# Hybrid decoder layer: sparse pairs begun among the u tiles, K=64 spreads of h2, gate rows on GpSimd, 56 dense columns

## The chip, the cores and the metric

One NeuronCore of a Trainium2 chip runs the whole layer in one launch. The metric is the device time of one execution in microseconds (us); the median of the runs is given.

## The reference, cut to what matters

The layer has a mixer (sparse attention and a short convolution) and then a retrieval FFN, called PEER. The change lies in the second half and in the load of one modulation vector, `gate2`.

```python
mod = silu(c) @ w_ada + b_ada          # shift1, scale1, gate1, shift2, scale2, gate2
...
h2 = rms_norm(x, norm2_w) * (1.0 + scale2) + shift2
x  = x + gate2 * peer_ffn(h2, ...)

# peer_ffn, for each of 256 tokens and 8 heads (16384 experts = 128 x 128):
q = h2 @ peer_wq                        # two halves of 128 a head
s = q . peer_subkeys                    # 128 scores for each half
vals, idx = top_k(s, 16)                # of each half
combo = vals0[:, None] + vals1[None, :] ; ids = idx0 * 128 + idx1
top_s, pos = top_k(combo, 16)           # 16 experts of the head
g = softmax(top_s)
a = gelu(peer_u[expert] . h2)           # rows of 1024
out = sum over heads and experts of g * a * peer_v[expert]
```

Each token so uses 8 x 16 = 128 experts, each with a row of `peer_u` and a row of `peer_v`, in float32.

## The kernel before

Expert e = 128 i + j has a column number j. The experts are split by j in two parts.

**Dense part, j < J0 = 64.** For each j, all 128 experts with that j are computed for all 256 tokens. `u_tile(j)` loads 512 KB of `peer_u` and multiplies it with `h2f` (h2 transposed, float32) on TensorE, 8 products of 128x128 by 128x256; ACT takes the GELU of it into `B0[:, j]` (`evict`, lines 1039 and 1042). `g_step` spreads the softmax weights of four tokens at a time (`GT = 4`, so 64 groups) over i and j: ACT and DVE make one-hot tiles `oi` and `oj` (lines 1074 to 1077), TensorE multiplies them (line 1065), DVE multiplies the result into `B0` (line 1055). One `g_step` follows each u tile; the groups left over are done in a loop behind the u tiles (lines 1194 to 1196). Then `v_tile(j)` loads 512 KB of `peer_v` and adds its product with `B0[:, j]` to the accumulators `po` in PSUM: two halves of tokens, each two products of 512 columns (line 1209). The *u stage* is the loop over u tiles, the *v stage* that over v tiles.

**Sparse part, j >= J0: the pairs.** For each token one indirect DMA on GpSimd's queue gathers, for its 128 experts on 128 partitions, rows of 8 KB (u and v side by side, line 1101). Experts with j < J0 get an index out of bounds and are not moved. Tokens go four at a time, a *quad*: 64 quads. In `pairs()` a quad has four *turns* (two tokens, one half of the 1024 columns): TensorE spreads the h2 row of a token over 128 partitions with a one-hot column `pick` (line 1139), DVE multiplies with the gathered u rows and sums (line 1142); after four turns ACT takes the GELU (1153), DVE puts in the weights (1154). `strips` multiplies with the gathered v rows into `po` (line 1113, 8 products, 16 instructions); it is placed in the third turn of the *next* quad and then calls `fetch()`, which issues the four gathers of the quad after that. The row buffers are a ring of nine.

h2 is kept in two float32r parts, high and low. The spread adds both: two products with K=32 for each token, `rh` and `rl`, written directly by `rows_of_h2` (ACT copies, DVE subtracts).

**What sets the order.** All instructions are laid out by hand. The retrieval (`retrieve(0)`, `retrieve(1)`: top-16 lists on DVE) and then the pairs are one generator, `stream()`, which is driven by a budget: `run(us)` adds `us` to `spent` and asks the generator for steps while `spent` is above zero; each step yields its price. `u_tile` calls `run(1.75)` twice, `v_tile` `run(1.72)` twice, the leftover loop `run(1.0)`. Other code changes `spent` for work that it adds. `pairs` waits for `po` to exist:

```python
            while len(po) <= tb:
                yield 1e6
```

and line 1201 sets `spent[0] = 0.0` ahead of the v stage. At the end of a retrieval, `fi` (indices and weights) is transposed on TensorE (line 974) and copied out; `state["T", tb]` lets the groups of these 128 tokens begin; `state["R"]` lets the buffers of the pairs be opened after the next u tile (line 1175): `p2` is closed, zeros are filled in on GpSimd (lines 1182 to 1187), `po[0]` and one pair of spread banks are taken, and two quads are fetched. A second pair of spread banks comes with the v stage.

**Loads.** `queue` holds the weight loads in order; SP issues each into one of three buffers `raw` (line 117). An item with a function as its second part is consumed by that function; others become operands, in the query stage (`queries()`, the products with `wq`) split by ACT and DVE into two parts (lines 121, 122). The eight loads of `w_ada[5]`, from which `gate2` is summed, stand among the u loads (j = 4, 6, ... 18), and DVE adds each (line 245).

Of the kernel before, what the change touches and what calls it, by code (L numbers as in the profile page):

```python
# [8 lines left out]
F32 = mybir.dt.float32  # L9
F32R = mybir.dt.float32r  # L10
# [8 lines left out]
L = 256  # L19
# [27 lines left out]
J0 = 64  # L47
# [3 lines left out]
ROWS = tuple(range(4, 20, 2))  # L51
# [45 lines left out]
def body(tc, i, out):  # L97
# [22 lines left out]
    def split(hi, lo, src):  # L120
        nc.scalar.copy(hi, src)  # L121
        nc.vector.tensor_tensor(lo, src, hi.bitcast(F32), op=OP.subtract)  # L122
# [120 lines left out]
    def add_row(acc, k):  # L243
        def use(raw):
            nc.vector.scalar_tensor_tensor(acc, raw, sc[:, k:k + 1], acc, op0=OP.mult, op1=OP.add)
        return use
# [46 lines left out]

    mk = [(m, k) for m in (1, 0) for k in range(KD)]
# [31 lines left out]
    W += [(i["wq"][hp].rearrange("p k c -> p (k c)"), None) for hp in range(16)]  # L326
# [12 lines left out]
    for j in range(J0):  # L339
        if j in ROWS:  # L340
            queue.append((i["w_ada"][5, ROWS.index(j)], add_row(gate2, ROWS.index(j))))
        queue.append((i["pu"][j].rearrange("p k c -> p (k c)"), None))
# [469 lines left out]
    iv = tr.tile([128, L], I32, name="iv")  # L812
    gp = tr.tile([128, L], F32, name="gp")
    pick = tr.tile([128, 128], F32R, name="pick")
    nc.scalar.copy(pick, ident)
    p2 = ExitStack()
    r1 = p2.enter_context(tc.tile_pool(name="r1", bufs=1))
    r2 = p2.enter_context(tc.tile_pool(name="r2", bufs=2))
    nc.gpsimd.tensor_tensor(h2f, h2h.bitcast(F32), h2l.bitcast(F32), op=OP.add)
# [3 lines left out]
    def rows_of_h2():  # L823

        h2r.extend(keep.tile([128, NT, D], F32R, name=n, tag=g) for n, g in (("rh", "h2h"), ("rl", "h2l")))
        for tb in TB:
            for g in range(2):
                pt = p_g.tile([128, 4, 128], F32, name="pg")
                for z in range(4):
                    nc.tensor.transpose(pt[:, z], h2f[:, g * 4 + z, TS[tb]], ident)  # L830
                s = slice(g * 512, g * 512 + 512)
                split(h2r[0][:, tb, s], h2r[1][:, tb, s], flat(pt))
# [68 lines left out]
    def retrieve(tb):  # L901
# [38 lines left out]
        for h in range(0, H, 2):  # L940
# [3 lines left out]
            for z in (h, h + 1):  # L944
# [17 lines left out]
        fi = r1.tile([128, 4, 128], F32, name="fi")  # L962
# [8 lines left out]
                                gs[:, :, None].to_broadcast([128, H, 16]), op=OP.mult)  # L971
        pt = p_acc.tile([128, 4, 128], F32, name="acc")
        for z in range(4):
            nc.tensor.transpose(pt[:, z], fi[:, z], ident)
        yield 1.0
# [6 lines left out]
        yield 0.4  # L982
# [10 lines left out]
    def stream():  # L993
        yield from cur
        while todo:
            yield from stage1(*todo.pop(0))
        yield from retrieve(0)
        yield from retrieve(1)
        state["R"] = True
        yield 0.1  # L1000
        yield from pairs()
# [3 lines left out]
    rows_of_h2()  # L1005
    gen = stream()
    spent = [0.0]

    def run(us):
        spent[0] += us  # L1010
        while spent[0] > 0:
            z = next(gen, None)
            if z is None:
                spent[0] = 0.0
                return
            spent[0] -= z

# [101 lines left out]
    def pairs():  # L1119
# [3 lines left out]
        for n in range(L // 4):  # L1123
            tb = n // 32
            c = n % 32
            while len(po) <= tb:
                yield 1e6
            rows = quads.pop(0)
            ah = wa2.tile([128, 2, 4], F32, name="ah")
            for q0 in (0, 2):  # L1130
                for d in range(2):
# [3 lines left out]
                    for part in range(2):  # L1135
                        for x in range(2):
                            p = slice((q0 + x) * 32, (q0 + x) * 32 + 32)
                            t = (q0 + x) * 32 + c
                            nc.tensor.matmul(bs[x], pick[p, t:t + 1].to_broadcast([32, 128]), h2r[part][p, tb, ds],  # L1139
                                             start=part == 0, stop=part == 1, tile_position=((q0 + x) * 32, 0))  # L1140
# [7 lines left out]
                    spent[0] += 0.45  # L1148
# [20 lines left out]
    for j in range(J0):  # L1169
# [5 lines left out]
        if state.pop("R", False):  # L1175
# [70 lines left out]
```

## Time and profile before

| | |
|---|---|
| median of 3 runs | 1260.73 us (1256.08 to 1268.48) |
| profiled execution | 1254.04 us |
| its span, first to last instruction | 1252.2 us |
| mean granted TensorE clock | 0.941 of full |
| busy: PE (TensorE products) | 1112.3 us, 89% |
| busy: DVE / ACT / POOL (GpSimd) | 764.3 / 295.6 / 293.1 us |
| moved by DMA | 255.98 MB, mean 204 GB/s |

Busy times are of the whole span; products are pipelined and overlap in the record, so a high share of PE does not say that it runs at its best rate. The clock is granted at one of two levels, full (2.4 GHz) or half (1.2 GHz); a window's number is the mean over it. Times in rows are us from the start of the span. "Idle before <- x" names what ended the wait ahead of an instruction.

### The profile page before, as it was taken

Reading aid. Unit: us, or ns where it says so; the run is one execution under the profiler, and the core shown is the slowest. Engines: PE = TensorE matmul, PEld = TensorE weight load, DVE = VectorE, ACT = ScalarE, POOL = GpSimd, SP = SyncE. Lnnn points to the kernel's source line nnn. Section 1 sums busy time; section 2 is a strip of 40 time slices with the busy share of each in tenths; the row PEclk is TensorE's granted clock in tenths of the full one; section 3 lists DMA queues with packets and bytes.
Section 4 is the critical chain, followed back from the end, with each engine's and each line's share of the span. In section 5 each row is a group of like instructions: output and inputs, shape, how many; then the busy total and the mean of one; then the engine's idle time right before and its main releaser. Section 6 shows DMA issues by size and latency. Waiting matters only on the chain. (4 is left out here: it accounts for less than half of the span.)

```text
span 1252.2 us, 16661 instructions
## 1 busy us (share of the span) xinstructions
PE 1112.3 (89%) x5644; PEld 677.1 (54%) x5644; DVE 764.3 (61%) x2341; ACT 295.6 (24%) x808; POOL 293.1 (23%) x295
## 2 busy tenths in 40 slices
PE   2899998996899999999989988988899988989887
PEld 1799878985789899986323333323333333333233
DVE  6697776889776433345555565555566655565561
ACT  2454534421466555564000000000000000000000
POOL 1000001004000600000333444333344334334330
PEclk9999988999899999997899899999899899899898
DMA  8675752434333633330677778687787777687672
GB/s 314 264 242 182 266 172 84 152 115 171 120 134 118 242 134 118 119 101 20 224 270 252 233 256 275 219 273 255 238 267 263 270 252 245 238 290 248 225 230 84
DMA packets 71316, 255.98 MB, mean 204 GB/s; under 512 B 24898, under 2 KB 24930, under 8 KB 55074
## 3 DMA queue, kind: packets, MB, share of 16 engines
q0 software_dynamic: 37104, 131.71, 32.0%
q1 hardware_dynamic: 33984, 122.18, 27.8%
q10 hardware_dynamic: 144, 1.05, 0.2%
q8 instruction: 44, 0.72, 0.2%
q14 instruction: 40, 0.33, 0.1%
HBM read 390.90 MB, written 1.05 MB: 313 GB/s over the span
## 5 line engine op out<-in xcount | busy, mean ns | idle before, releaser
L1101 POOL DMA_INDIRECT uv<-in_uv_dram,iv x256 | 253.3, 989 | 540.2 <-PE acc L1113 320.6
L1142 DVE CUSTOM_DVE_ANT_0 junk<-uv,acc 128x512 f32<-128x512 f32 x256 | 176.0, 687 | 182.3 <-DMA uv<-in_uv_dram,iv 129.8
L1029 PE MATMUL mm<-h2f,raw 128*128 128x256 f32 x1024 | 237.3, 386 | 2.8 <-DMA raw<-in_pu_dram 2.4
L1142 DVE CUSTOM_DVE_ANT_0 junk<-uv,pg 128x512 f32<-128x512 f32 x256 | 176.1, 688 | 62.2 <-PE pg L1139 13.9
L1029 PEld LDWEIGHTS mm<-h2f,raw 128*128 128x128 f32 x1024 | 192.6, 193 | 30.0 <-issue 4.7
L1153 ACT ACTIVATE gx<-gx 128x4 f32<-128x4 f32 x64 | 13.1, 205 | 627.1 <-DVE gx L1152 528.2
L1139 PE MATMUL acc<-rh,pick 32*128 32x512 f32 x256 | 99.6, 507 | 64.7 <-DVE ah L1142 61.4
L1209 PE MATMUL acc<-raw,B 128*128 128x512 f32 x256 | 137.7, 664 | 0.0
L1209 PE MATMUL mm<-raw,B 128*128 128x512 f32 x256 | 137.0, 661 | 0.0
L1139 PEld LDWEIGHTS acc<-rh,pick 32*128 32x128 f32 x256 | 37.1, 185 | 154.9 <-DVE ah L1142 115.8
L1139 PEld LDWEIGHTS pg<-rh,pick 32*128 32x128 f32 x256 | 27.3, 189 | 105.0 <-DVE ah L1142 68.5
L1074 ACT ACTIVATE oi<-iota,Ti 128x128 f32<-128x128 f32 x256 | 81.6, 391 | 1.3 <-PE pg L1065 1.3
L122 DVE TENSOR_TENSOR hl<-raw,hl 128x1024 fp32r<-128x1024 f32 x46 | 60.6, 1321 | 33.1 <-ACT hl L121 32.7
L1209 PEld LDWEIGHTS acc<-raw,B 128*128 128x128 f32 x256 | 47.1, 203 | 61.4 <-issue 61.4
L1065 PEld LDWEIGHTS pg<-oj,oi 128*128 128x128 f32 x512 | 73.2, 211 | 11.4 <-ACT oi L1077 8.7
L1065 PE MATMUL pg<-oj,oi 128*128 128x64 f32 x512 | 72.5, 291 | 6.7 <-ACT oi L1077 6.7
L1209 PEld LDWEIGHTS mm<-raw,B 128*128 128x128 f32 x256 | 46.4, 200 | 58.6 <-issue 58.6
L1139 PE MATMUL acc<-rl,pick 32*128 32x512 f32 x256 | 77.8, 438 | 0.0
L1043 DVE TENSOR_TENSOR B<-B,ge 128x4 f32<-128x4 f32 (+50 forms) x51 | 13.6, 267 | 103.0 <-ACT ge L1042 100.2
L1139 PE MATMUL pg<-rh,pick 32*128 32x512 f32 x256 | 70.5, 506 | 3.4 <-DVE ah L1142 2.4
L1113 PE MATMUL mm<-uv,z 128*32 128x512 f32 x512 | 67.9, 652 | 3.5 <-DVE z L1154 3.5
L1113 PE MATMUL acc<-uv,z 128*32 128x512 f32 x512 | 66.2, 637 | 0.0
(253 smaller groups left out, 1506.5 us busy)
## 6 DMA issues: line engine op xcount, KB each, us to landing
raw<-in_pu_dram SPq DMA_DIRECT2D x64, 512.0 KB
raw<-in_pv_dram SPq DMA_DIRECT2D x64, 512.0 KB
raw<-in_w_ada_dram SPq DMA_DIRECT2D x48, 512.0 KB
raw<-in_wq_dram SPq DMA_DIRECT2D x16, 512.0 KB
raw<-in_w_c_dram SPq DMA_DIRECT2D x12, 512.0 KB
raw<-in_w_kv_dram SPq DMA_DIRECT2D x8, 512.0 KB
raw<-in_w_out_dram SPq DMA_DIRECT2D x8, 512.0 KB
uv<-in_uv_dram,iv POOLq DMA_INDIRECT x256
```

Of the source, the lines that this page charges most:

```text
L122: nc.vector.tensor_tensor(lo, src, hi.bitcast(F32), op=OP.subtract)
L1029: nc.tensor.matmul(ps, w[0][:, k * 128:k * 128 + 128], h2f[:, k], start=k == 0, stop=k == KD - 1)
L1043: nc.vector.tensor_tensor(b[:, :n], b[:, :n], ge[:, :n], op=OP.mult)
L1065: nc.tensor.matmul(ps[:, n], oi[:, n], oj[:, n], start=True, stop=True)
L1074: nc.scalar.activation(out=oi[:, n], in_=iota, func=AF.Square, bias=Ti[:, t:t + 1])
L1101: nc.gpsimd.indirect_dma_start(out=rows[q], out_offset=None, in_=i["uv"], in_offset=bass.IndirectOffsetOnAxis(ap=iv[:, t:t + 1], axis=0), ...
L1113: nc.tensor.matmul(po[tb][d][q * 32:q * 32 + 32], z[:, q, 31 - c:63 - c], rows[q][:, D + d * 512:D + d * 512 + 512], start=False, stop=not ...
L1139: nc.tensor.matmul(bs[x], pick[p, t:t + 1].to_broadcast([32, 128]), h2r[part][p, tb, ds], start=part == 0, stop=part == 1, tile_position=( ...
L1142: nc.vector.tensor_tensor_reduce(out=junk, in0=rows[q0 + x][:, ds], in1=bs[x], scale=1.0, scalar=0.0, op0=OP.mult, op1=OP.add, accum_out=a ...
L1153: nc.scalar.activation(out=ge, in_=ge, func=AF.Gelu_apprx_tanh)
L1209: nc.tensor.matmul(po[tb][d], B0[:, j, TS[tb]], v[0][:, d * 512:d * 512 + 512], start=False, stop=not parts[tb])
```

## The change

Five things are edited.

1. `yield 1e6` and the flag `R` go; the stream yields `None` until the pairs' buffers are open (`not po`), and `run` then ends its call. The pairs begin in the u stage. A turn is priced at 1.55 with 0.3 (0.45 before) given back.
2. The transposes and copies at the end of a retrieval become `spread_out`, put into a list `later` that `run` works off one call or more further on.
3. `rows_of_h2` splits into a temporary `hl`, and 16 DMAs on GpSimd's queue put high and low part of 32 tokens under each other on 64 partitions. A spread is then one product with K=64 for each token.
4. The eight gate rows stand among the query loads, and `pool_row` multiplies and adds them on GpSimd.
5. J0 is 56: eight u tiles and v tiles fewer, and 72 instead of 64 columns of experts are gathered.

```diff
-J0 = 64
+J0 = 56
-ROWS = tuple(range(4, 20, 2))
...
+    def pool_row(acc, k):
+        def use(raw):
+            nc.gpsimd.tensor_scalar(raw, raw, sc[:, k:k + 1], None, op0=OP.mult)
+            nc.gpsimd.tensor_tensor(acc, acc, raw, op=OP.add)
+        return use
...
-    W += [(i["wq"][hp].rearrange("p k c -> p (k c)"), None) for hp in range(16)]
+    for hp in range(16):
+        W.append((i["wq"][hp].rearrange("p k c -> p (k c)"), None))
+        if hp % 2 == 0:
+            W.append((i["w_ada"][5, hp // 2], pool_row(gate2, hp // 2)))
...
     for j in range(J0):
-        if j in ROWS:
-            queue.append((i["w_ada"][5, ROWS.index(j)], add_row(gate2, ROWS.index(j))))
         queue.append((i["pu"][j].rearrange("p k c -> p (k c)"), None))
...
-    def rows_of_h2():
+    def rows_of_h2(tb):
...
-                split(h2r[0][:, tb, s], h2r[1][:, tb, s], flat(pt))
+            split(hl[:, 0, s], hl[:, 1, s], flat(pt))
+        for q in range(4):
+            for part in range(2):
+                p = (q % 2) * 64 + part * 32
+                nc.gpsimd.dma_start(out=h2r[q // 2][p:p + 32, tb], in_=hl[q * 32:q * 32 + 32, part])
...
+        yield 1.0
+        later.append([1, lambda: spread_out(tb, fi)])
+
+    def spread_out(tb, fi):
         pt = p_acc.tile([128, 4, 128], F32, name="acc")
         for z in range(4):
             nc.tensor.transpose(pt[:, z], fi[:, z], ident)
-        yield 1.0
...
-        yield 0.4
+        spent[0] -= 0.4
         state["T", tb] = True
...
         yield from retrieve(1)
-        state["R"] = True
-        yield 0.1
+        while not po:
+            yield None
         yield from pairs()
...
             z = next(gen, None)
             if z is None:
                 spent[0] = 0.0
                 return
             spent[0] -= z
+        while later and later[0][0] <= 0:
+            later.pop(0)[1]()
+        if later:
+            later[0][0] -= 1
...
             while len(po) <= tb:
-                yield 1e6
+                yield None
...
-                    for part in range(2):
-                        for x in range(2):
-                            p = slice((q0 + x) * 32, (q0 + x) * 32 + 32)
-                            t = (q0 + x) * 32 + c
-                            nc.tensor.matmul(bs[x], pick[p, t:t + 1].to_broadcast([32, 128]), h2r[part][p, tb, ds],
-                                             start=part == 0, stop=part == 1, tile_position=((q0 + x) * 32, 0))
+                    for x in range(2):
+                        p = slice(x * 64, x * 64 + 64)
+                        nc.tensor.matmul(bs[x], pick[p, c:c + 1].to_broadcast([64, 128]), h2r[q0 // 2][p, tb, ds],
+                                         start=True, stop=True, tile_position=(x * 64, 0))
...
-                    spent[0] += 0.45
+                    spent[0] += 0.3
                     yield 1.55
...
-        if state.pop("R", False):
+        if not po and state.get(("T", 1)):
             p2.close()
```

## Rows read from the trace of the kernel before

**Rows 1.** Windows: busy us (and instructions) of each engine, granted clock, DMA share, GB/s.
```profile
420.00:440.00 20.00, 20.00 (x109) 18.04 (x109) 6.29 (x27) 11.50 (x37) 8.37 (x9) 1.00 0.92 341
600.00:1200.00 600.00, 532.74 (x2342) 187.91 (x2341) 350.00 (x1076) 12.33 (x60) 236.24 (x240) 0.92 0.76 254
230.00:240.00 10.00, 10.00 (x88) 10.00 (x86) 8.95 (x39) 5.07 (x9) 0.00 (x0) 1.00 0.46 160
```

**Rows 2.** Timeline, 710 to 720 us, all engines: start, duration, instruction, idle before it.
```profile
710.21 0.99 POOL L1101 DMA_INDIRECT uv<-in_uv_dram,iv  x1 [3.71 <-DVE ah L1142]
...
710.55 1.98 PE L1209 MATMUL acc<-raw,B 128*128 128x512 f32 x4
...
712.47 0.49 PE L1139 MATMUL acc<-rh,pick 32*128 32x512 f32 x2
...
713.03 0.39 PE L1139 MATMUL pg<-rh,pick 32*128 32x512 f32 x2
...
715.42 0.69 DVE L1142 CUSTOM_DVE_ANT_0 junk<-uv,acc 128x512 f32<-128x512 f32 x1 [1.38 <-DMA uv<-in_uv_dram,iv]
...
716.82 1.92 PE L1113 MATMUL acc<-uv,z 128*32 128x512 f32 x16
...
719.00 0.99 POOL L1101 DMA_INDIRECT uv<-in_uv_dram,iv  x1 [3.92 <-PE acc L1113]
```

**Rows 3.** Line 1153, the GELU of a quad: durations, first and last start.
```profile
L1153 ACT ACTIVATE gx<-gx x64: 205/205/207, 591.5 to 1221.2; 128x4 f32<-128x4 f32 x64
```

**Rows 4.** Windows of 3 us around a wait for gathers.
```profile
775.00:778.00 3.00, 0.57 (x3) 0.18 (x1) 1.24 (x3) 0.00 (x0) 2.39 (x3) 0.94 0.86 303
...
781.00:784.00 3.00, 3.00 (x7) 0.83 (x5) 0.87 (x4) 0.00 (x0) 0.00 (x0) 0.50 0.83 336
```

**Rows 5.** Line 1029, the u tiles, and the timeline of TensorE at 315 us.
```profile
L1029 PE MATMUL mm<-h2f,raw x1024: 379/379/634, 261.4 to 552.8; 128*128 128x256 f32 x171
...
315.04 1.20 PE L974 MATMUL acc<-ident,fi 128*128 128x128 f32 x3 [9.56 <-DVE fi L963]
```

**Rows 6.** Timeline of TensorE, end of the u stage to the first v tile.
```profile
545.18 3.67 PE L1029 MATMUL mm<-h2f,raw 128*128 128x256 f32 x16
...
549.53 3.67 PE L1029 MATMUL mm<-h2f,raw 128*128 128x256 f32 x16
...
553.04 1.89 PE L1065 MATMUL pg<-oj,oi 128*128 128x64 f32 x16
...
577.49 3.02 PE L712 MATMUL mm<-gate,ones 128*128 128x512 f32 x4
...
582.14 1.88 PE L1209 MATMUL acc<-raw,B 128*128 128x512 f32 x4
```

**Rows 7.** GpSimd: fills, gathers (lines 1187, 1101) and the sum of line 819.
```profile
L1187 POOL MEMSET uv<- x6: 1799/1846/1957, 408.2 to 417.3; 128x2048 f32 x6
...
L1101 POOL DMA_INDIRECT uv<-in_uv_dram,iv x256: 984/990/1109, 419.3 to 1211.7; - x128
...
196.49 4.51 POOL L819 TENSOR_TENSOR h2f<-h2h,h2l 128x2048 f32<-128x2048 f32 x1 [48.38 <-DVE h2l L122]
```

**Rows 8.** Timeline: two query tiles on ACT, two gate rows, GpSimd beside one.
```profile
217.48 0.37 ACT L888 COPY pqT<-mm 128x256 f32<-128x256 f32 x1
...
220.79 0.37 ACT L888 COPY pqT<-mm 128x256 f32<-128x256 f32 x1
...
268.46 0.33 SPq L117 DMA_DIRECT2D raw<-in_w_ada_dram  x1
...
272.02 1.28 DVE L245 SCALAR_TENSOR_TENSOR gate<-raw,sc,gate 128x1024 f32<-128x1024 f32 x1 [0.71 <-DMA raw<-in_w_ada_dram]
...
287.26 5.02 POOL L949 TENSOR_TENSOR eq<-eq,ce 128x800 f32<-128x800 f32 x2 [86.25 <-DVE eq L947]
...
288.55 2.14 DVE L245 SCALAR_TENSOR_TENSOR gate<-raw,sc,gate 128x1024 f32<-128x1024 f32 x1
```

**Rows 9.** The page's part 3: the queue of the gathers, packets, MB, share.
```profile
q0 software_dynamic: 37104, 131.71, 32.0%
```

**Rows 10.** The chain that ended last: the first step of `finish`.
```profile
1243.36 0.70 DVE raw L1216
```

More of the change, by code (lines that the diff above doesn't have):

```diff
@@ L811, in body @@
     Tg = tr.tile([128, L], F32, name="Tg")
[L812 to L815, printed above, removed]
     p2 = ExitStack()
@@ L818, in body @@
     r2 = p2.enter_context(tc.tile_pool(name="r2", bufs=2))
+    iv = tr.tile([128, L], I32, name="iv")
+    gp = tr.tile([128, L], F32, name="gp")
+    pick = tr.tile([128, 32], F32R, name="pick")
+    pk = r1.tile([128, 32], F32, name="pk")
+    nc.vector.tensor_tensor(pk, ident[:, 0:32], ident[:, 32:64], op=OP.add)
+    nc.vector.tensor_tensor(pk, pk, ident[:, 64:96], op=OP.add)
+    nc.vector.tensor_tensor(pick, pk, ident[:, 96:128], op=OP.add)
     nc.gpsimd.tensor_tensor(h2f, h2h.bitcast(F32), h2l.bitcast(F32), op=OP.add)
     h2r = []
-    def rows_of_h2():
[L825 to L831, printed above, removed]
-                split(h2r[0][:, tb, s], h2r[1][:, tb, s], flat(pt))
+    def rows_of_h2(tb):
+        if not tb:
+            h2r.extend(keep.tile([128, NT, D], F32R, name=n, tag=g) for n, g in (("r0", "h2h"), ("r1", "h2l")))
+        hl = halves.tile([128, 2, D], F32R, name="hl")
+        for g in range(2):
+            pt = p_g.tile([128, 4, 128], F32, name="pg")
+            for z in range(4):
+                nc.tensor.transpose(pt[:, z], h2f[:, g * 4 + z, TS[tb]], ident)
+            s = slice(g * 512, g * 512 + 512)
+            split(hl[:, 0, s], hl[:, 1, s], flat(pt))
[3 more added lines that the diff above has]
+                nc.gpsimd.dma_start(out=h2r[q // 2][p:p + 32, tb], in_=hl[q * 32:q * 32 + 32, part])
     skT = r1.tile([128, 16, 128], F32, name="skT")
@@ L961, in retrieve @@
         nc.vector.tensor_scalar(ei, ei, 127, None, op0=OP.bitwise_and)
-        fi = r1.tile([128, 4, 128], F32, name="fi")
+        fi = r1.tile([128, 4, 128], F32, name=f"fi{tb}")
         nc.vector.tensor_copy(fi[:, 0], ih)
@@ L1004, in body @@
     queries()
-    rows_of_h2()
+    for tb in TB:
+        rows_of_h2(tb)
     gen = stream()
     spent = [0.0]
+    later = []
     def run(us):
```

## The prediction

> **What bounds the kernel now.** I read the windows first, stage by stage, and then one stretch of the timeline of the longest stage, instruction by instruction. From 600 to 1200 us the engines do the sparse pairs and the v tiles. TensorE is down as busy for 533 of these 600 us, DVE for 350, and the DMA engines carry 254 GB/s at a share of 0.76 [rows 1]. A busy TensorE looks like the bound, but its instructions are few per quad. The timeline gives their full-clock prices: a spread turn 0.56 us (from 712.47 to 713.03), half a v tile 1.92 us (710.55 to 712.47), and the 16 strip products of a quad 1.92 us [rows 2]. A quad (four tokens) has four turns and one set of strips. By the kernel's own budget (`yield` and `spent`) it costs 4 x (1.55 - 0.45) + 0.4 - 1.72 = 3.08, and a v tile gives 2 x 1.72 = 3.44, so 1.79 halves of v tiles go with a quad. That is 2.24 + 1.92 + 3.44 = 7.6 us of products. The mean quad takes (1221.2 - 591.5) / 63 = 10.0 us [rows 3], so 2.4 us per quad is something else.
>
> That something is a ring of nine row buffers. A quad's four gathers are issued after the strips of the quad two before it. Its first gather goes out at 710.21 [rows 2], DVE waits 1.38 us for the second row and takes it at 715.42, TensorE then spreads and starts the strips at 716.82, and the next gather leaves at 719.00: a loop of 8.8 us at full clock. The quads average 10.0 rather than 8.8 because the clock halves at times: after 775 to 778, in which TensorE is busy for 0.57 of 3 us, the granted clock reads 0.50 at 781 to 784 [rows 4], which is the 1.2 GHz level. Over 600 to 1200 us it averages 0.92 [rows 1], so about a sixth of that time is at half clock. So the v stage is bound by gather latency and transfer, then the clock, and not by the sum of products.
>
> Ahead of it lies the u stage, 261.4 to 553 us [rows 5]. Its tiles take 4.35 us (545.18 to 549.53) [rows 6] with TensorE full, and no pair work is in it: `pairs` meets `yield 1e6`, which puts the budget out of reach until line 1201 resets it. The eight gathers issued at 419.3 [rows 7] lie unused until the v stage begins at 582 [rows 6].
>
> **The change, part by part.**
>
> *Pairs in the u stage.* With `yield None` the pairs start in the tile after their pools are opened. A tile gives 2 x 1.75 and pays 0.35 + 0.35 + 1.1 for group work: 1.7 net. A quad now costs 4 x (1.55 - 0.30) + 0.4 - 1.72 = 3.68. The second retrieval ends in the same tile by the budget (30 of 0 to 55), and `later` adds two tiles, so the pools open after tile 32 (31 before). Tiles 33 to 55 give 23 x 1.7 / 3.68 = 10.6 quads; 56 v tiles give 56 x 3.44 / 3.68 = 52.3; the last quad runs after the v tiles.
>
> *Time of opening.* Before, TensorE stood 9.56 us at 315.04 because the transposes of `retrieve(0)` waited for DVE [rows 5]. Two edits take from this. Of the eight gate rows, five lie ahead of it on DVE, three like the one at 272.02 (1.28 us) and two like that at 288.55 (2.14 us) [rows 8], 8.1 us in all; and `later` puts the transposes a tile further on in TensorE's order. DVE would be done near 307 instead of 315, and TensorE by then has done one tile more (some 3.5 us): 12 us won. The other three rows win nothing here: TensorE is not held up by DVE in this way again before 408. The opening was at 408.2 [rows 7]; it becomes 408.2 + 4.35 - 12 = 400, plus 2 for the next item, 402.
>
> *Gate rows on GpSimd in the query stage.* Each row now takes two GpSimd passes over 128x1024. The trace has no such multiply by a column: a fill of twice the size takes 1.85 us, and an addition of twice the size 4.51 us [rows 7], so a pass lies between 0.92 and 2.26 us, and a row, which has an addition in it, between 3.2 and 4.5 us. Loads go w, row, w, w, row, so with three buffers a row always follows a row in the same buffer, and its load lands 3.5 us after issue (268.46 to 272.02) [rows 8]. A turn of that buffer takes 6.7 to 8 us. A query tile takes 3.31 us (217.48 to 220.79) [rows 8], two of them 6.6 us. So SP, which must keep the order, holds the query weights back by 0 to 1.4 us per row; 0 to 9 us over the stage, less what is already loaded ahead. I take 2. GpSimd's other work (the sum `h2f`, the sixteen new copies of h2's parts, the products of `retrieve(0)`) moves behind the rows; the copies are wanted only 140 us later, and the products were first wanted at 287.26, by when 16 issues at about a gather's 0.99 us each [rows 7] from 262 on are nearly done. What GpSimd does to DVE is seen too: a gate row of 1.28 us took 2.14 us beside GpSimd's product at 287.26 [rows 8]. DVE is busy 8.95 of 10 us in the query stage [rows 1], so it can absorb about 6 us of such stretching; that stands inside the 9.
> The Trainium skill (GPSIMD Engine Reference, section 8, Key points) says that GpSimd shares SBUF interfaces with VectorE and contends with DVE instructions that have two SBUF inputs; the trace agrees, with 2.14 against 1.28 us. By that rule alone DVE would give back in the query stage the 8 us that it wins later, and the forecast would be 1182 instead of 1174.
>
> *u tiles 33 to 55.* 23 x 4.35 = 100 us, plus 10.3 quads x (4 x 0.28 + 1.92) = 31 us of products, taking a K=64 turn as half of the old one (one product per token instead of two; a turn is between 0.28 and 0.56 us). New waits: the first turn is placed in the next tile, but GpSimd fills six buffers first, 408.2 to 419.3 [rows 7], and the second row needs 5 us more. DVE stands some 12 us, behind it `oj` and the B products; TensorE has a tile or so in hand, so it loses about 7. With one pair of spread banks in this stage, and gathers and u loads at (2.32 + 2.1 x 0.52) MB per 12.5 us = 273 GB/s, I add 5 (0 to 45). End of the stage: 402 + 143 = 545, against 553.
>
> *The loop that finishes the groups.* Fewer u tiles leave more groups over: 13 steps before, from 553.2 to 577.5 [rows 6], 1.87 us each; 56 u tiles with groups from tile 12 on leave 22 steps, 41 us. Its budget is 1.0 - 0.35 - 1.1 < 0 per step, so no pairs run in it. To the first v tile 4.6 us more [rows 6]: 591, against 582. Dropping eight u tiles thus does not end this stage earlier.
>
> *v stage.* 52 quads instead of 64. A quad's gathers grow by 72/64, from 131.7/64 = 2.06 [rows 9] to 2.32 MB, and 1.07 v tiles (0.56 MB) go with it instead of 0.9: 2.88 MB instead of 2.53. In that loop [rows 2] two of four rows land before DVE goes on, at 2.06 / 4 MB and 254 GB/s 2.0 us a row, so an eighth of 4 us more, +0.5, while the shorter spread takes off 0.28: 10.0 becomes 10.2. If instead time goes with bytes, 10.0 x 2.88 / 2.53 = 11.4. The best rate shown, 341 GB/s [rows 1], would allow 8.4, and if no quad met a slow clock the loop would give 9.0. I take 10.7, between latency and bytes, as transfers of one quad touch the next: 52 x 10.7 = 556, ending at 1147. TensorE's own 1.12 + 1.92 + 4.1 = 7.1 us per quad stays hidden.
>
> *End.* The last quad alone: DVE's 350/60 = 5.8 us of work [rows 1] with gaps, GELU and strips, about 10. From DVE's first step of `finish` at 1243.36 to the span's 1252.2 is 9 us [rows 10]. Span 1166, execution 1168 against 1254.0, 6.9% less. The shown median, 1260.7, lies 0.5% above the profiled execution, so I forecast a median of 1174.
>
> **The rivals.**
> 1. *Bytes rule* (11.4 us per quad): 1174 + 36 = 1210. For it: the share is already 0.76. Against: 0.92 was reached at 420 to 440.
> 2. *Latency only, fewer slow quads* (9.3): 1174 - 73 = 1101. For it: the loop of 8.8 [rows 2]. Against: the same loop averages 10.0 today.
> 3. *The u stage stalls*: in-order DVE waits for rows, `oj` comes late, and TensorE loses a further 40 us: 1214.
> 4. *It doesn't do what it says*: `run` returns on None without looking at `later`, so if a tile's group costs did not exceed 1.75, retrieval 1 would never be spread out, or much later. They are 1.8, by a hair. With pairs only from the v stage on, 11.7 quads are left behind the v tiles, at 9 us each: 502 + 46 + 556 + 11.7 x 9 + 9 = 1218, 1227 as a median.
> 5. *Half clock takes the v stage* (slower). TensorE has less to do per quad and waits longer, and after such a wait the clock reads 0.50 [rows 4]. If it held throughout, products would take 14.3 us per quad: +187, 1360. It turns the sign from a mean of 12.5 us, that is with over half of the quads at half clock, a granted clock below about 0.73; today 0.92.
> The Trainium skill (TensorE: Matmul & The Clock Gate, section HAM oscillation) speaks for rival 5: gaps between bursts of matmuls put the engine back to half rate each time. The trace agrees after the gap at 775, with 0.50.
>
> **How the numbers follow.** Forecast (10.0 to 11.1 us per quad, 1140 to 1200): 0.50. Rival 1 or 3 (1200 to 1235): 0.20. Rival 2 (1095 to 1140): 0.18. Rivals 1 and 3 together, 1174 + 36 + 40 = 1250: 0.05. Rival 4: 0.02. Rival 5: 0.05. The range 1112 to 1228 leaves out rival 5, the two together, and the outer ends of 1, 2 and 3. One per cent, about what a measurement of this kernel tells from no change, is 13 us: faster than 1248 has 0.50 + 0.20 + 0.18 + 0.02 = 0.90, within it 0.05 (rivals 1 and 3 together), slower 0.05.
>
> **What would show it.** Right: first spread product near 405 us, u stage ending near 545, 22 group steps, the first v tile near 591, GELU of the pairs spaced 10.7 us there. The stall of 9.56 us gone. Wrong: a spread turn still near 0.56 us; quads over 11.4 us; a granted clock under 0.8 after 600; long DVE waits for gathers ahead of 545; query tiles spaced by more than 3.3 us.

## The result and the profile after

The changed kernel takes 1204.51 us (median of three runs, 1201.12 to 1208.39) against 1260.73: a ratio of 0.955, with an interval of 0.946 to 0.964. The forecast was 1174, in a range of 1112 to 1228. So the direction held and the gain was two thirds of the one forecast: 4.5% instead of 6.9%. The profiled execution has a span of 1206.7 us, against a forecast of 1166; the stage times below are of that execution.

The page of the changed kernel (span, busy times, the gather queue as in [rows 9]) and, from its list of groups of instructions, two, with the idle time ahead of them and what ended it:
```profile
span 1206.7 us, 15237 instructions
PE 1031.5 (85%) x4940; PEld 632.3 (52%) x4940; DVE 751.5 (62%) x2327; ACT 285.4 (24%) x781; POOL 350.4 (29%) x327
...
q0 software_dynamic: 37872, 155.21, 38.0%
...
L120 ACT CAST hl<-raw 128x1024 fp32r<-128x1024 f32 x46 | 47.8, 1046 | 59.5 <-DMA raw<-in_wq_dram 41.0 <-DMA raw<-in_w_out_dram 4.5 <-DMA raw<-in_w_iq_dram 4.5
...
L295 POOL TENSOR_SCALAR raw<-raw,sc 128x1024 f32<-128x1024 f32 x8 | 30.6, 3830 | 50.5 <-DMA raw<-in_w_ada_dram 40.2 <-issue 10.3
```
The eight GpSimd multiplies of a gate row take 3.83 us each on average, and ACT, which splits the query weights as they come, stood 41.0 us waiting for these weights.

Windows of the changed kernel, in the columns of [rows 1] (length; busy time of TensorE's products, TensorE's weight loads, DVE, ACT and GpSimd; granted clock; DMA share; GB/s): the query stage, the first spread turn of the u stage, the rest of that stage, the loop that finishes the groups, 600 to 1200 us as in [rows 1], and the v stage:
```profile
230.00:240.00 10.00, 8.39 (x56) 8.19 (x56) 5.82 (x26) 2.90 (x6) 5.95 (x2) 0.83 0.33 118
430.00:440.00 10.00, 2.04 (x5) 1.10 (x5) 2.41 (x7) 0.00 (x0) 7.56 (x9) 0.50 0.88 271
441.00:607.00 166.00, 149.96 (x752) 104.04 (x752) 87.29 (x311) 54.18 (x192) 35.73 (x36) 0.93 0.62 212
609.00:650.00 41.00, 39.10 (x164) 36.35 (x164) 25.17 (x99) 35.84 (x96) 0.00 (x0) 0.50 0.01 4
600.00:1200.00 600.00, 517.02 (x1953) 199.93 (x1955) 347.22 (x1091) 53.98 (x173) 210.85 (x214) 0.90 0.75 261
660.00:1150.00 490.00, 421.91 (x1571) 142.00 (x1569) 282.65 (x871) 10.06 (x49) 190.94 (x194) 0.94 0.83 292
```
In the query stage TensorE is busy for 8.39 of 10 us, where it was full before, and DVE for 5.82 instead of 8.95 [rows 1]. The group loop runs at a granted clock of 0.50, the 1.2 GHz level, with the DMA engines idle. In the v stage they carry 292 GB/s.

The lines of the changed kernel that give the stages (min/median/max ns, first and last start us; the last line is the GELU of a quad, as in [rows 3]):
```profile
L1052 PE MATMUL mm<-h2f,raw x896: 378/379/797, 279.1 to 602.3; 128*128 128x256 f32 x180
...
L295 POOL TENSOR_SCALAR raw<-raw,sc x8: 3517/3669/4863, 172.6 to 265.2; 128x1024 f32<-128x1024 f32 x8
...
L296 POOL TENSOR_TENSOR gate<-gate,raw x8: 2371/2395/2407, 176.7 to 268.9; 128x1024 f32<-128x1024 f32 x8
...
L1208 POOL MEMSET uv<- x6: 1798/1802/1950, 418.4 to 427.3; 128x2048 f32 x6
...
L1230 PE MATMUL acc<-raw,B x224: 592/593/1222, 654.0 to 1177.0; 128*128 128x512 f32 x112
...
L1174 ACT ACTIVATE gx<-gx x64: 188/205/207, 453.3 to 1197.6; 128x4 f32<-128x4 f32 x64
```
Beside [rows 5 to 7] the u tiles begin 17.7 us later (279.1 against 261.4), the pools open 10.2 us later (418.4 against 408.2), the first v tile starts 71.9 us later (654.0 against 582.1), and the last GELU comes 23.6 us earlier.

The timeline of the changed kernel in the query stage, at the opening and in the v stage (start, duration, engine; in brackets the idle time before it and what ended it):
```profile
220.00 3.66 POOL L295 TENSOR_SCALAR raw<-raw,sc 128x1024 f32<-128x1024 f32 x1 [5.17 <-issue]
...
223.74 2.37 POOL L296 TENSOR_TENSOR gate<-gate,raw 128x1024 f32<-128x1024 f32 x1
...
231.16 3.57 POOL L295 TENSOR_SCALAR raw<-raw,sc 128x1024 f32<-128x1024 f32 x1 [5.05 <-DMA raw<-in_w_ada_dram]
...
418.38 10.73 POOL L1208 MEMSET uv<- 128x2048 f32 x6 [93.16 <-PE acc L992]
...
425.89 0.49 PE L1160 MATMUL acc<-r,pick 64*128 64x512 f32 x2
...
429.28 1.11 POOL L1124 DMA_INDIRECT uv<-in_uv_dram,iv  x1 [0.18 <-issue]
...
435.14 0.69 DVE L1163 CUSTOM_DVE_ANT_0 junk<-uv,acc 128x512 f32<-128x512 f32 x1 [13.02 <-DMA uv<-in_uv_dram,iv]
...
435.89 0.79 PE L1160 MATMUL acc<-r,pick 64*128 64x512 f32 x1 [9.51 <-DVE ah L1163]
...
438.75 0.79 PE L1160 MATMUL acc<-r,pick 64*128 64x512 f32 x1 [2.07 <-DVE ah L1163]
...
441.22 4.86 PE L1052 MATMUL mm<-h2f,raw 128*128 128x256 f32 x16
...
661.49 0.20 ACT L1174 ACTIVATE gx<-gx 128x4 f32<-128x4 f32 x1 [8.47 <-DVE gx L1173]
...
702.71 0.49 PE L1160 MATMUL pg<-r,pick 64*128 64x512 f32 x2
703.13 1.98 PE L1230 MATMUL mm<-raw,B 128*128 128x512 f32 x4
...
709.42 0.99 POOL L1124 DMA_INDIRECT uv<-in_uv_dram,iv  x1 [4.26 <-PE acc L1136]
710.82 0.69 DVE L1163 CUSTOM_DVE_ANT_0 junk<-uv,acc 128x512 f32<-128x512 f32 x1 [1.56 <-DMA uv<-in_uv_dram,iv]
...
719.06 0.99 POOL L1124 DMA_INDIRECT uv<-in_uv_dram,iv  x1 [4.77 <-PE acc L1136]
...
1197.56 0.21 ACT L1174 ACTIVATE gx<-gx 128x4 f32<-128x4 f32 x1 [9.10 <-DVE gx L1173]
```
A gate row takes GpSimd 6.0 us, then GpSimd stands 5.05 us for the load of the next one: 11.2 us from row to row. At the opening the first spread starts at 425.89, but GpSimd fills buffers until 429, and DVE gets the first row nearly 6 us after its issue (429.28 to 435.14). TensorE, in order behind DVE, takes its next u product at 441.22. In the v stage the ring is as in [rows 2]: gathers wait for the strips, DVE for a row, and the loop from the first gather behind one quad's strips to that behind the next quad's is 9.6 us (709.42 to 719.06). By their order these are not the first gathers of their quads: nine buffers hold two quads and one row, so the four gathers behind a set of strips are the second, third and fourth row of one quad and the first of the next. A spread turn takes 0.42 us (702.71 to 703.13).

### The profile page after: what moved, and what is told of

The parts are those of the page before. It is cut to its first block, busy times and chain, and to the rows that moved or that the text cites. A ratio compares the mean times of both kernels' runs of the same rounds, so it can differ in the third digit from the quotient of the medians.

```text
span 1206.7 us, 15237 instructions
## 1 busy us (share of the span) xinstructions
PE 1031.5 (85%) x4940; PEld 632.3 (52%) x4940; DVE 751.5 (62%) x2327; ACT 285.4 (24%) x781; POOL 350.4 (29%) x327
## 3 DMA queue, kind: packets, MB, share of 16 engines
q0 software_dynamic: 37872, 155.21, 38.0%
## 5 line engine op out<-in xcount | busy, mean ns | idle before, releaser
L1163 DVE CUSTOM_DVE_ANT_0 junk<-uv,acc 128x512 f32<-128x512 f32 x296 | 203.6, 688 | 248.7 <-DMA uv<-in_uv_dram,iv 146.9
L1052 PE MATMUL mm<-h2f,raw 128*128 128x256 f32 x896 | 212.8, 394 | 10.6 <-ACT B L1062 5.1
L1160 PE MATMUL acc<-r,pick 64*128 64x512 f32 x296 | 107.6, 499 | 90.8 <-DVE ah L1163 90.4
L1163 DVE CUSTOM_DVE_ANT_0 junk<-uv,pg 128x512 f32<-128x512 f32 x216 | 148.6, 688 | 48.7 <-PE pg L1160 20.1
L1160 PEld LDWEIGHTS acc<-r,pick 64*128 64x128 f32 x296 | 41.1, 187 | 195.3 <-DVE ah L1163 155.9
L1088 PE MATMUL pg<-oj,oi 128*128 128x56 f32 x512 | 86.8, 329 | 5.3 <-ACT oi L1100 5.3
L1160 PEld LDWEIGHTS pg<-r,pick 64*128 64x128 f32 x216 | 22.8, 192 | 94.5 <-DVE ah L1163 68.5
L1160 PE MATMUL pg<-r,pick 64*128 64x512 f32 x216 | 60.1, 513 | 5.0 <-DVE ah L1163 4.8
L1098 DVE TENSOR_SCALAR oj<-iota,Tj,Tg 128x56 f32<-128x56 f32 x256 | 63.2, 316 | 0.0
L120 ACT CAST hl<-raw 128x1024 fp32r<-128x1024 f32 x46 | 47.8, 1046 | 59.5 <-DMA raw<-in_wq_dram 41.0
```

Source lines behind the costliest of these rows:

```text
L1052: nc.tensor.matmul(ps, w[0][:, k * 128:k * 128 + 128], h2f[:, k], start=k == 0, stop=k == KD - 1)
L1088: nc.tensor.matmul(ps[:, n], oi[:, n], oj[:, n], start=True, stop=True)
L1098: nc.vector.tensor_scalar(oj[:, n], iota[:, :J0], Tj[:, t:t + 1], Tg[:, t:t + 1], op0=OP.is_equal, op1=OP.mult)
L1160: nc.tensor.matmul(bs[x], pick[p, c:c + 1].to_broadcast([64, 128]), h2r[q0 // 2][p, tb, ds], start=True, stop=True, tile_position=(x * 64, 0))
L1163: nc.vector.tensor_tensor_reduce(out=junk, in0=rows[q0 + x][:, ds], in1=bs[x], scale=1.0, scalar=0.0, op0=OP.mult, op1=OP.add, accum_out=a ...
```

## The experiments

Each is the changed kernel with one edit; two combinations stand under the seventh. Stage times of the profiled executions, in us; "per quad" is the mean distance of two GELUs from the first one in the v stage to the last; the ratio is to the kernel before, run beside it, with its interval.

| kernel | first u product | pools open | first v product | per quad | last GELU | span | median | ratio |
|---|---|---|---|---|---|---|---|---|
| before | 261.4 | 408.2 | 582.1 | 10.00 | 1221.2 | 1252.2 | 1260.73 | 1 |
| changed | 279.1 | 418.4 | 654.0 | 10.11 | 1197.6 | 1206.7 | 1204.51 | 0.955 (0.946 to 0.964) |
| e1_rows_dve | 257.8 | 401.9 | 635.0 | 10.11 | 1178.1 | 1187.2 | 1184.91 | 0.942 (0.937 to 0.947) |
| e2_fill_dve | 277.7 | 419.6 | 649.5 | 10.04 | 1188.8 | 1197.9 | 1204.93 | 0.961 (0.956 to 0.967) |
| e3_loop_pairs | 276.8 | 416.0 | 685.5 | 10.26 | 1194.8 | 1215.4 | 1219.74 | 0.973 (0.968 to 0.978) |
| e4_pairs_v | 280.8 | 420.0 | 572.2 | 10.15 | 1220.8 | 1229.9 | 1233.65 | 0.985 (0.978 to 0.991) |
| e5_k32 | 279.9 | 419.4 | 665.1 | 10.54 | 1231.7 | 1240.8 | 1238.30 | 0.986 (0.977 to 0.996) |
| e6_j64 | 277.3 | 416.6 | 693.9 | 9.69 | 1177.9 | 1222.8 | 1227.92 | 0.983 (0.972 to 0.992) |
| e7_evict | 281.5 | 421.3 | 649.7 | 10.05 | 1189.8 | 1198.9 | 1198.77 | 0.957 (0.947 to 0.967) |
| e9_half_rows | 276.6 | 415.9 | 644.3 | 8.87 | 1122.0 | 1131.1 | 1140.02 | 0.912 (0.904 to 0.920) |
| e12_half_reduce | 281.4 | 420.7 | 645.0 | 9.95 | 1178.3 | 1187.4 | 1189.12 (one run) | beside one run of 1253.35 |

**Gate rows back on DVE, among the u loads.**
```diff
-            W.append((i["w_ada"][5, hp // 2], pool_row(gate2, hp // 2)))
...
+ROWS = tuple(range(14, 30, 2))
+        if j in ROWS:
+            queue.append((i["w_ada"][5, ROWS.index(j)], add_row(gate2, ROWS.index(j))))
```


> Gate rows back on DVE, one pass each, among u tiles 14 to 28; all else as in the changed kernel. Theory (the GpSimd rows, 6.2 us of passes and 3.5 to 4 us of load in one buffer per two query tiles, stretch the query stage by 18 us): the first u tile starts near 261 instead of 279 and the kernel takes about 1204 - 16 = 1188. Rival (the query stage is longer because of the sixteen copies of h2 or the extra loads, or DVE is what the retrieval waits for anyway): the u tiles start after 270, or what is won there is lost again ahead of the opening, and the time stays within 1198 to 1205.

The line of the u products in this kernel:
```profile
L1053 PE MATMUL mm<-h2f,raw x896: 379/379/794, 257.8 to 583.0; 128*128 128x256 f32 x180
```
Its window of the query stage:
```profile
230.00:240.00 10.00, 10.00 (x87) 10.00 (x86) 8.44 (x37) 5.08 (x9) 0.00 (x0) 1.00 0.45 159
```
TensorE is full in the query stage again (10.00 against 8.39) and the u tiles begin 21.3 us earlier. Some 5 us of that go in the u tiles: from the first u product to the tile after the opening it is 148.1 us (to 405.93) instead of 143.2 (to 422.34). The span is 19.5 us shorter. The two ratios' intervals just touch (0.947 and 0.946), so the size of the gain is uncertain, but the stage at which it arises is not: the rows in the query stage cost the queries some 20 us. This run moves both the place of the loads and the engine; rows on DVE among the query loads were not run. The timeline above says what holds the loads there: a row's buffer is free only after GpSimd's two passes, 6.0 us, and the next row comes 5.05 us later.

**Buffers filled by DVE instead of GpSimd.**
```diff
-                nc.gpsimd.memset(uvp.tile([128, 2 * D], F32, name="uv"), 0.0)
+                nc.vector.memset(uvp.tile([128, 2 * D], F32, name="uv"), 0.0)
```


> The six zero fills of the row buffers on DVE instead of GpSimd; all else as in the changed kernel. Theory (the first gathers stand behind 11 us of fills in GpSimd's order, DVE waits for them in the first turn, and TensorE loses 15 us behind it): the wait of 13 us on DVE falls below 6, the time to about 1196. Rival (the wait is that of the gathers themselves, whatever stands ahead of them): the wait stays above 10 us and the time within 1201 to 1207.

The fills in the timeline of this kernel, and the spread behind them:
```profile
430.31 1.76 DVE L1208 MEMSET uv<- 128x2048 f32 x1 [0.38 <-issue]
...
432.68 1.62 PE L1160 MATMUL acc<-r,pick 64*128 64x512 f32 x2 [7.62 <-DVE ah L1163]
```
DVE's fills take 1.76 us, hardly less than GpSimd's 1.80, and they stand ahead of the first product with a row on that engine. TensorE's wait shrinks from 9.5 + 2.1 to 7.6 us, and the time doesn't change measurably. Another engine doesn't hide the fills; making them earlier was not tried.

**Pairs in the loop that finishes the groups.**
```diff
-        run(1.0)
+        run(2.2)
```


> The loop that finishes the groups gets a budget of 2.2 instead of 1.0 per step, so that four to five quads run in it; all else as in the changed kernel. Theory (in these 44 us DMA stands still, and the v stage is paced by gathers at 10.1 us a quad): the loop grows by up to 10 us, the v stage loses four quads, 40 us, and keeps three or four v tiles bare at its end, 13 us: about 1185. Rival (in-order waits in ACT and DVE stretch the loop by as much as the v stage wins): 1200 to 1208.

Window of that loop in this kernel:
```profile
606.00:684.00 78.00, 64.60 (x266) 40.50 (x266) 48.08 (x176) 37.65 (x103) 15.95 (x16) 0.59 0.36 116
```
Slower. The DMA engines are no longer idle there (116 GB/s instead of 4), but the loop grows by more than 30 us at a clock of 0.59. From the end of the u products to the first v product TensorE is busy for 68.9 us instead of 46.0, and stands 16.6 us instead of 5.3, 7.6 of it for `oj`, which DVE makes between its rows. Four quads more are done before the v stage, and from its first product to the end of the span that stage takes 529.9 us instead of 552.7: 23 us won, less than the loop lost. It is no longer the quads that end it: the last GELU comes at 1194.8, and v tiles run on alone to 1209.

**Pairs from the v stage on only.**
```diff
-        while not po:
+        while len(po) < 2:
```


> The pairs wait for the v stage as they did before; all else as in the changed kernel. Theory (the u stage pays some 85 us for its ten and a half quads, 15 at the start and the rest as tiles of 7.5 instead of 4.35 us, and these quads cost 9 to 10 us each behind the v tiles): u stage 85 us shorter, 11.7 quads left over, 110 us, time about 1225. Rival 1 (the early quads are worth nothing, their stalls eat it all): 1200 to 1208. Rival 2 (as forecast, quads of the u stage cost only their products): 1245 or more.

Windows of the u stage and of the end in this kernel:
```profile
441.00:523.00 82.00, 81.73 (x451) 73.86 (x451) 28.79 (x114) 46.02 (x152) 1.37 (x2) 1.00 0.45 165
1090.00:1215.00 125.00, 83.12 (x276) 24.33 (x278) 69.09 (x213) 2.47 (x12) 46.48 (x47) 0.62 0.67 222
```
The u stage ends 79 us earlier (its last tile starts at 523.3 instead of 602.3). But the v tiles end at 1085.5, and the last twelve GELUs follow (1220.8 - 1093.4) / 12 = 10.6 us apart, with nothing beside them and a clock of 0.62. Early quads are worth about 3% net in this order of work. With v tiles beside them the quads of this kernel take (1084.0 - 581.4) / 50 = 10.05 us. So taking the v tiles away doesn't shorten a quad; the clock fell with them, so what they cost at a full clock isn't shown.

**Two products with K=32 in place of one with K=64.** This keeps the parts of h2 in two tiles, without the sixteen copies.
```diff
-                        nc.tensor.matmul(bs[x], pick[p, c:c + 1].to_broadcast([64, 128]), h2r[q0 // 2][p, tb, ds],
-                                         start=True, stop=True, tile_position=(x * 64, 0))
+                    for part in range(2):
...
+                            nc.tensor.matmul(bs[x], pick[p, t:t + 1].to_broadcast([32, 128]), h2r[part][p, tb, ds],
+                                             start=part == 0, stop=part == 1, tile_position=((q0 + x) * 32, 0))
```


> The second part undone alone: two K=32 products per token from two full tiles, written without copies; budgets and all else as in the changed kernel. Theory (a turn costs 0.23 us more, on the gather loop of the v stage and among the u tiles, where TensorE is the pace): 52 quads with one such turn on the loop, 12 us, and 42 turns in the u stage, 10 us: about 1225. Rival (TensorE waits for rows anyway, the spread lies in these waits): 1200 to 1208.

The timeline of a turn and the v half behind it in this kernel:
```profile
702.42 0.73 PE L1154 MATMUL pg<-r,pick 32*128 32x512 f32 x4
703.08 1.98 PE L1224 MATMUL mm<-raw,B 128*128 128x512 f32 x4
```
Per quad 10.54 instead of 10.11 us, the first v tile 11 us later, and 34 us in all. K=64 is thus worth about as much as the early quads. A full-clock turn ahead of a v half takes 0.66 us here (702.42 to 703.08) and 0.42 us with K=64. Four turns save 0.96 us of TensorE, and of that 0.43 comes through to the quad, more than the 0.28 that I had counted.

**64 dense j.**
```diff
-J0 = 56
+J0 = 64
```


> The fifth part undone alone: 64 dense columns; all else as in the changed kernel. Theory (stages add up: eight more u tiles at 7.5 us with three and a half more quads in them, +60, eight steps of the group loop less, -16, 50 quads at 9.8 us and some ten bare v tiles at 3.5 us in the v stage instead of 53 quads at 10.1, -10): about 1238. Rival (the columns only move work from dense tiles to gathers, bytes and all): 1200 to 1210.

The v stage after the last quad in this kernel:
```profile
1180.00:1214.00 34.00, 34.00 (x79) 14.86 (x76) 0.12 (x1) 0.00 (x0) 0.00 (x0) 0.95 0.32 108
```
Rows of 64 instead of 72 gathered columns: 9.69 us per quad instead of 10.11. The queue of the gathers moves 133.81 MB here and 155.21 in the changed kernel, the 2.10 MB of h2's copies in both, so the change brings 16% more gathered bytes, and they cost 0.42 us per quad. But the first v tile comes 40 us later, and v tiles run on alone for 38 us after the last quad. Over all, 56 is some 23 us better here.

**B's eviction after the fourth of the next tile's eight products, rather than after that tile.**
```diff
+            if k == 3 and late is not None:
+                evict(late)
...
-        ps = u_tile(j)
-        if late is not None:
-            evict(late)
-        late = ps
+        late = u_tile(j)
```


> In the u stage the GELU of the tile before is placed between the two halves of a tile's products, ahead of the pair work, instead of behind it; all else as in the changed kernel. Theory (a u tile takes 7.5 us partly because ACT takes the GELU of a quad, for which it waits for DVE, ahead of the u tile's, and TensorE's next tile waits 1.4 us for a bank): that wait is gone in about half of the 22 tiles, some 15 us, time about 1190. Rival (only the single pair of spread banks and DVE hold the u stage): 1200 to 1207.

From the opening to the first v tile it is 228.4 us instead of 235.6, but the time, 0.957 (0.947 to 0.967), can't be told from that of the changed kernel. With the gate rows on DVE as well it gave 1187.62 us, 0.945 (0.939 to 0.950), no better than those rows alone:

> The gate rows on DVE among u tiles 14 to 28 and the earlier GELU of the u tiles together. Theory (both save time of the stages ahead of the v stage, which is 10.1 us a quad whatever lies ahead): 16 + 6 us less than the changed kernel, about 1181, ratio to the kernel before near 0.938. Rival (the second is hidden once the first has moved DVE's work): 1185 to 1190, as with the rows alone.

The same with a v tile's budget raised gave 0.951 (0.944 to 0.957), again no gain:
```diff
-            run(1.72)
+            run(1.8)
```


> As the run before, and the v tiles give a budget of 2 x 1.8 instead of 2 x 1.72, so that 54.8 quads go with the 56 v tiles instead of 52.3 and none is left behind them. Theory (the last two quads run alone behind the v tiles, at 9 us each with TensorE nearly idle; spread among the v tiles they cost what a quad's gathers cost, but the v tiles no longer stretch it): the v tiles and the pairs end together, some 5 to 8 us less than the run before. Rival (a quad's period does not depend on how many v tiles go with it, so that the number of quads alone counts): the same time as the run before, within 3 us.

**Half of the bytes of each gather.**
```diff
-        nc.vector.tensor_scalar(fi[:, 2], fi[:, 1], float(J0), SKIP, op0=OP.is_lt, op1=OP.mult)
+        nc.vector.tensor_scalar(fi[:, 2], fi[:, 1], 92.0, SKIP, op0=OP.is_lt, op1=OP.mult)
```


> Only experts of columns 92 and up are gathered, half of the rows and bytes; the others' products are made with old rows of the buffers, so the output leaves them out. Theory (the v stage goes by the loop of latency, DVE and products, and by the clock, not by bytes): two rows land 1.1 us sooner, so a quad takes about 9.0 instead of 10.1 us, the whole 1204 - 60 = 1144. Rival (bytes rule): a quad falls to the 7.3 us of DVE's own work, the whole to 1060 or less; at the other end no gain at all (1190 or more) if only DVE and TensorE count.

Window of the v stage in this kernel, beside the row of 660 to 1150 above:
```profile
660.00:1090.00 430.00, 399.38 (x1573) 137.22 (x1573) 284.63 (x877) 10.06 (x49) 191.32 (x194) 0.97 0.63 200
```
Half the gathered bytes take a quad from 10.11 to 8.87 us, 12% less, while the rate falls to 200 GB/s. Time going with bytes would have given far less than 8.87, and bytes without effect 10.1. A loop of latency with a transfer in it is what fits, and the time, 1140, came out near the theory's 1144.

**Half of the width of DVE's product and sum.**
```diff
+                        hs = slice(d * 512, d * 512 + 256)
-                        nc.vector.tensor_tensor_reduce(out=junk, in0=rows[q0 + x][:, ds], in1=bs[x], scale=1.0,
+                        nc.vector.tensor_tensor_reduce(out=junk[:, :256], in0=rows[q0 + x][:, hs], in1=bs[x][:, :256], scale=1.0,
```


> DVE reduces 256 of the 512 columns of every turn and the output leaves out the rest, so that the one pair of spread banks of the u stage comes free in about 1 us instead of 1.7; all else as in the changed kernel. Theory (from 441 to 607 us the 22 u tiles take 7.5 instead of 5.8 us by three things: spreads at 0.6 us a turn while TensorE waits for DVE to free the banks, waits of 16 us, and half clock behind them): the 22 tiles take 15 us less, some 150 us; the v stage, in which DVE's second reduce of a turn lies on the gather loop, falls to about 9.5 us a quad; the whole some 1155. Rival (TensorE's products alone are dearer beside each other, DVE is not waited for): 22 tiles within 4 us of 166, and a quad of the v stage at 10.0 or more.

Windows of the u stage from the first turn on, and of the v stage, in this kernel:
```profile
441.00:592.70 151.70, 142.35 (x749) 100.58 (x748) 65.30 (x306) 52.89 (x186) 37.03 (x38) 0.97 0.66 228
660.00:1130.00 470.00, 407.96 (x1527) 138.43 (x1526) 175.47 (x844) 9.65 (x47) 184.80 (x187) 0.94 0.84 297
```
In the v stage DVE's busy share falls from 282.65 / 490 = 0.58 to 175.47 / 470 = 0.37, but a quad only from 10.11 to 9.95 us. I had counted DVE's part of the loop in full; that fell. What DVE no longer works it waits for rows. Its waits from 660 to 1130 us (total, times, longest), in the changed kernel and in this one:
```profile
DVE junk L1163 <- DMA uv<-in_uv_dram,iv: 113.8, 79, 4.7
...
DVE junk L1164 <- DMA uv<-in_uv_dram,iv: 190.8, 116, 5.0
```
In the u stage the last tile starts 150 us after 442.7, against 161 after 441.2. Of these 11 us, 4 are less waiting of TensorE (9.4 us instead of 13.2); the rest are shorter products at a clock of 0.98 instead of 0.93. That the clock was higher because of DVE's shorter work isn't shown by one run.

The traces also divide the loop of a quad, from the gather of its second row to DVE's first product with that row, and from there to the next quad's second gather (means of quads 17 to 60, us):

| kernel | gather to product | product to next gather |
|---|---|---|
| before | 5.63 | 4.44 |
| changed | 6.09 | 4.05 |
| e5_k32 | 6.13 | 4.52 |
| e6_j64 | 5.74 | 3.86 |
| e9_half_rows | 5.05 | 3.82 |
| e12_half_reduce | 6.29 | 3.79 |

K=64 shortens the second part; fewer bytes shorten mostly the first; what half of DVE's work takes off the second, the first in part takes back.

## Why the prediction held, and where it was short

The sum of the span, term by term:

| term | forecast | measured | difference |
|---|---|---|---|
| first u product | 263 | 279.1 | +16 |
| to the opening | 139 | 139.3 | 0 |
| opening to the end of the u tiles | 143 | 188.8 (to 607.2) | +46 |
| group loop to the first v tile | 46 | 46.8 | +1 |
| v stage to the last GELU | 566 | 543.6 | -22 |
| finish | 9 | 9.1 | 0 |
| span | 1166 | 1206.7 | +41 |

The direction held and the time lies in the range, but not where the forecast had put it: 1204.5 is in the stretch of rival 1 or 3 (1200 to 1235), which had a chance of 0.20. And the range held in part by luck: without the 22 us that the v stage gave back, the median would have been about 1227, just inside it.

**The gate rows in the query stage** were the first mis-sized term: +2, with bounds of 0 and 9, measured +17.7. I priced a multiply by a column from a fill and an addition [rows 7], 0.92 to 2.26 us; it takes 3.83 us, more than the two-input addition behind it (2.39). A row so takes 6.0 to 6.2 us instead of 3.2 to 4.5, and its load 5.05 us instead of 3.5, so the cycle of two query tiles is 11.2 us instead of 6.6. The sign that I named, query tiles spaced by more than 3.3 us, is there as ACT's 41.0 us of waiting for query weights, and gate rows back on DVE take it away. It is the queue far more than contention: DVE is busy for only 5.82 of 10 us there. Of its sixteen subtractions for the query weights, three more than in the kernel before were stretched, from 1.23 to between 2.05 and 2.80 us, 3.7 us in all, and all before 216 us. The Trainium skill (GPSIMD Engine Reference, section 8, Key points) has GpSimd contend with DVE instructions that have two SBUF inputs; the trace agrees in these three, but the one at 222.42, beside GpSimd's multiply, kept its 1.23 us, and the 8 us that DVE was to give back by that rule did not come.

**The stall of `retrieve(0)`** came out right in sum, partly by luck. The 9.56 us [rows 5] are gone, and the opening comes 139.3 us after the first u product, where 139 was forecast. But TensorE's waits in this stretch fell by 9.7 us (16.1 to 6.4) instead of 12, with a new one of 5.1 us for an eviction by ACT at 327.6, which I hadn't seen coming, and the rest of the stretch grew by 2.2 us where I had counted a tile, 4.35. How the gain divides between the gate rows and `later` wasn't run apart.

**The u tiles with pairs** were the second mis-sized term, and the largest: +46. The opening fell in the middle of a tile (+4, to the next tile at 422.34). The first turn cost 15 us (425.9 to 441.2), not 7. The other 22 tiles took 166 us instead of 130. Of those, the windows of single lines give the spreads as 23.6 us for 39 turns, 0.60 each instead of 0.28, and the strips as 20.4; u and group products take 88.07 + 25.45 = 113.5 instead of 96 (their records overlap a little with others); TensorE stood 16 us instead of 5, at a clock of 0.93. My bounds for a turn, 0.28 to 0.56, held at full clock: it takes 0.42, and I had taken the low end. Rival 3 (1214) came near in price, but by its mechanism only at the first turn, where DVE waits 13 us for the first row. Waits in the 22 tiles, 441 to 607 us (total, times, longest):
```profile
PE acc L1160 <- DVE ah L1163: 9.0, 16, 0.8
...
PE mm L1052 <- ACT ge L1065: 4.1, 3, 1.4
...
DVE junk L1163 <- DMA uv<-in_uv_dram,iv: 3.1, 1, 3.1
```
DVE waits only once for a row there, and TensorE never for `oj`: it waits for DVE to free the spread banks, and for ACT. Of the 36 us too many in these tiles, 11 are waits and some 5.5 the dearer turns (39 times 0.14). The clock, by an estimate, made 12: a mean of 0.93 is half clock for 14% of 166 us, 23 us, in which products take twice as long. The rest, and what made the clock fall so often, wasn't taken apart; half-width work on DVE gives 11 us of the 36 back.

**The group loop** came as forecast: 22 steps, about 2.0 us each, with no pairs. Pairs in it, at the one budget that was run, cost more than they gained, so its idle DMA engines are no easy gain.

**The v stage** was over-sized by 22 us, which hid half of the error ahead of it. I took 10.7 us per quad, between a latency end of 10.2 and a bytes end of 11.4; it is (1197.56 - 661.49) / 53 = 10.11. The latency end was right, and both of its parts stand on runs: eight more columns cost 0.42 us (forecast 0.5), and K=64 gives 0.43 (forecast 0.28). Two steps to it were not right. The gather at 710.21 [rows 2] is that of a quad's second row, so one row's landing lies on the loop and not two; and the bytes grew by 16%, not by the eighth of 72/64. The two errors work against each other. Nor does the half clock explain by itself why the mean lies above the one loop that was read: of the 51 distances of GELUs beside v tiles in the changed kernel, the 26 with a full clock throughout average 10.26 us, the other 25 10.05. In the kernel before, 35 at full clock average 9.45, not 8.8, and the other 28 10.67. Rival 1, the bytes rule, is out by the half-size gathers. Rival 2, latency without slow quads, is out too: the clock was 0.94 there and the quads no nearer to 9.3.

**The rivals of failure** didn't come about. Rival 4 is refuted by the spread at 425.89; pairs from the v stage on alone would have given 1233.65, against 1227 forecast for it. For rival 5 a clock below 0.73 was needed, and from 600 to 1200 us, the group loop in it, it was 0.90, from 660 to 1150 us 0.94. It does come where quads run bare: 0.62 in e4's last stretch. Of the signs of being wrong, three showed: the spaced query tiles, DVE's wait of 13 us for a gather ahead of the v stage, and turns of 0.60 us in the u stage, though 0.42 at full clock.

The fastest version run that computes the whole output is the changed kernel with the gate rows left on DVE: 1184.91 us, 0.942 of the kernel before. The same with the earlier eviction, 1187.62, can't be told from it.

## What to carry to other kernels

Price a moved operation by a row of the same form on the engine where it will run; where there is none, let the upper bound reach beyond the nearest dearer-looking row, and ask which loads queue behind it. Work put into a stage where TensorE is full pays its products and, on top, the waits and the lower clock that come with its order: here 22 tiles cost 36 us more than the sum of products and allowance. In a stage set by a ring of buffers, halve the bytes and halve the suspected engine's work separately before trusting either: here the bytes gave 12% and DVE's work under 2%, although the DMA engines were at a share of 0.83 and DVE at 0.58. And know which row of which quad a gather in the timeline belongs to before reading a loop off it.

## What was unexpected of the hardware

- GpSimd's multiply of 128x1024 f32 by a per-partition column takes 3.83 us (median 3.67), and its addition of two such tiles 2.39 us: the operation with one tensor input is the slower one.
- A fill of 128x2048 f32 takes 1.76 us on DVE and 1.80 us on GpSimd.
- Four `oj` operations of 128x56 that took 0.96 us together took 2.53 us beside GpSimd's fills at 419.59.
- After the wait of 9.51 us at the opening the granted clock read 0.50 from 430 to 440. The Trainium skill (TensorE: Matmul & The Clock Gate, section HAM oscillation) has a gap between bursts of products put the engine back to half rate; this trace agrees.
- In the group loop the clock stayed at 0.50 although TensorE's products fill 39.10 of 41 us; ahead of it lay a wait of 3.39 us for ACT. Why it stayed down isn't shown.
- Bare quads, at a clock of 0.62, took 10.6 us each, and quads with a v tile beside them 10.05 in the same kernel.
